# One of the last five output pieces of a hybrid block: scaled by ScalarE and added in DRAM onto an early written residual

## The chip, the cores and the metric

The kernel runs on one core of one Trainium2 chip. The metric is the time of one execution on the device in microseconds (us), the median of several runs. A profile of one execution goes with it; all times within the execution are counted from the start of its span.

## What is computed

One layer (DEPTH = 1) of an encoder block on 256 tokens of width 2048, in float32. What matters here is its frame and its last lines:

```python
mix = hybrid_mixer(u, ...)                       # three branches, then m @ w_out
x = x + _rms_norm(mix, norm_mix_post[l])         # the residual x1
hdn = jnp.square(jax.nn.relu(_rms_norm(x, norm_mlp_pre[l]) @ w_mlp_up[l]))
x = x + _rms_norm(hdn @ w_mlp_down[l], norm_mlp_post[l])
```

The output is therefore x1 + y * g4 * r4, where y is the product of the second half of the MLP, g4 the gain of the last norm (one number per column) and r4 the reciprocal root of y's mean square (one number per token).

## The kernel before, in words

Two token tiles (tt = 0 and 1) of 128 tokens each lie on the 128 partitions. All weights come from one DRAM array, wst, in pieces of 128x1024 (512 KB) loaded by SyncE's queue (L162) into three buffers, `raw`; ScalarE makes a rounded copy `whi` (L173), VectorE the rest `wlo` (L175), and TensorE multiplies with both.

The residual x1 (two tiles of 128x2048) is finished in the middle of the program, when the output projection of the mixer is done: `add_mixed` (L1115, VectorE) adds the normed mix to x in pieces of 512 columns. Right behind, `turn` (L1140, TensorE) transposes each piece, `cut` (L1156 on ScalarE, L1154 on VectorE) scales it by the next norm's gain and splits it, and `part` and `rest` (L1167, L1173, TensorE) begin the MLP's first product with it. In this stretch the order of each engine's instructions is written out by hand.

After that x1 is read for its squares (L1305) and then again only at the end. During most of the MLP, GpSimd issues 56 adding transfers from one SBUF tile to another (`dma_add`, L1358), which add 512 KB onto a buffer that is already filled.

The end of the kernel is the loop over four groups g of 512 columns (its body is L1520 to L1534). `tok` gives the last product of the group for tile 0 and then for tile 1. VectorE adds it to y (L1522), ScalarE squares and sums (L1523), VectorE multiplies by the gain (L1526). In the last group r4 follows (`rstd_of`): ScalarE scales the sum (L1095) and GpSimd takes the power -0.5 (L1096). With r4 the output is made in five pieces of 512, 512, 512, 256 and 256 columns, each one instruction on VectorE (L1532, y * r4 + x1, written over x1) and one transfer to DRAM (L1533). Pieces 0, 2 and 4 are sent by SyncE's queue, pieces 1 and 3 by ScalarE's:

```python
for c, w in (0, 512), (512, 512), (1024, 512), (1536, 256), (1792, 256):
    cs = slice(c, c + w)
    V.scalar_tensor_tensor(x1[tt][:, cs], ys[tt][:, cs], r4, x1[tt][:, cs], ALU.mult, ALU.add)
    (nc.scalar if c == 512 or w == 256 and c == 1536 else nc.sync).dma_start(
        out=out[tt * 128:tt * 128 + 128, cs], in_=x1[tt][:, cs])
```

Outside the stretches that are written out by hand a scheduler sets each engine's order from the dependencies and the order in which the code was written, and assigns a semaphore to each DMA in turn. `junk()` gives one of two 128x512 scratch tiles. At the end SyncE waits for all DMAs that are still under way, and the engines meet (L1655).

Of the kernel before, what the change touches and what calls it, by code (L numbers as in the profile page):

```python
# [13 lines left out]
AF = mybir.ActivationFunctionType  # L14
ALU = mybir.AluOpType
# [37 lines left out]
def hybrid_block(ctx, tc, xt, x, gains, params, consts, lora, gup, wst, out):  # L53
    nc = tc.nc
    V, A, G, PE = nc.vector, nc.scalar, nc.gpsimd, nc.tensor
# [10 lines left out]
    def nm(s):  # L66
        uid[0] += 1
        return f"{s}_{uid[0]}"
# [139 lines left out]
    def tok(pks, lag=1, mid=()):  # L208


        ps = [gps(), gps()]
        n = len(pks)
        kept = []

        def prod(hl, k0, tt):
            for w, parts in ((hl[0], (0, T)), (hl[1], (0,))):
                for k in (k0, k0 + 1):
                    for part in parts:
                        c = part + tt * 128
                        PE.matmul(ps[tt], pks[k][:, c:c + 128], w[:, (k - k0) * 512:(k - k0) * 512 + 512],  # L220
                                  start=k == 0 and part == 0 and w is hl[0], stop=w is hl[1] and k == n - 1)

        for k0 in range(0, n, 2):
            hl = wnext()
            if k0 >= n - 2 * lag:
                prod(hl, k0, 0)
                kept.append((hl, k0))
                tick()
                continue
            for w, parts in ((hl[0], (0, T)), (hl[1], (0,))):  # L230
                for k in (k0, k0 + 1):
                    for tt in range(2):
                        for part in parts:
                            c = part + tt * 128
                            PE.matmul(ps[tt], pks[k][:, c:c + 128], w[:, (k - k0) * 512:(k - k0) * 512 + 512],  # L235
                                      start=k == 0 and part == 0 and w is hl[0], stop=False)
                    if w is hl[1] or k == k0:
                        tick(0.7 if w is hl[0] else 0.5)
        yield ps[0]
        for i, (hl, k0) in enumerate(kept):  # L240
            prod(hl, k0, 1)
            tick()
            if i < len(mid):
                mid[i]()
        yield ps[1]
# [841 lines left out]
    def rstd_of(ss, eps, sums):  # L1087

        if sums is None:
            sums = cpool.tile([128, 1], F32, name=nm("ssum"))  # L1090
            V.tensor_reduce(sums, ss[:, 0:3], AX.X, ALU.add)
            V.tensor_scalar(sums, sums, 1.0 / D, eps, ALU.mult, ALU.add)
            return sums
        r = cpool.tile([128, 1], F32, name=nm("rs"))
        A.activation(r, ss[:, 3:4], AF.Identity, scale=1.0 / D, bias=sums)  # L1095
        G.tensor_tensor(r, r, cst[:, 2:3], ALU.pow)  # L1096
        return r
# [5 lines left out]
    x1 = [p2.tile([128, D], F32, tag="x1", name=nm("x1"), bufs=2) for _ in range(2)]  # L1103
    for c in range(0, D, 512):
        for tt in range(2):
            loads.append(lambda tt=tt, c=c: nc.sync.dma_start(out=x1[tt][:, c:c + 512],
                                                              in_=x[tt * 128:tt * 128 + 128, c:c + 512]))
# [3 lines left out]
    def junk():  # L1111
        return p2.tile([128, 512], F32, tag="junk", name=nm("junk"), bufs=2)
# [174 lines left out]
    ys = []  # L1287
# [227 lines left out]
        return [p3.tile([128, HALF], F32, tag="raw2", name=nm("kw"), bufs=6).bitcast(F32R) for _ in range(2)]  # L1515

    home[0] = spare
    for g in range(4):
        gs = slice(512 * g, 512 * g + 512)
        for tt, ps in enumerate(tok(hp, 4 if g == 3 else 1)):  # L1520
            yv = ys[tt][:, gs]
            V.tensor_tensor(yv, yv, ps, ALU.add)  # L1522
            A.activation(junk(), yv, AF.Square, accum_out=ss4[:, tt, g:g + 1])  # L1523
            if g == 3:
                r4 = rstd_of(ss4[:, tt, :], None, sum4[tt])
            V.tensor_tensor(yv, yv, g4[g], ALU.mult)  # L1526
            if g == 2:
                sum4.append(rstd_of(ss4[:, tt, :], eps4[tt], None))
            if g == 3:
                for c, w in (0, 512), (512, 512), (1024, 512), (1536, 256), (1792, 256):  # L1530
                    cs = slice(c, c + w)
                    V.scalar_tensor_tensor(x1[tt][:, cs], ys[tt][:, cs], r4, x1[tt][:, cs], ALU.mult, ALU.add)  # L1532
                    (nc.scalar if c == 512 or w == 256 and c == 1536 else nc.sync).dma_start(  # L1533
                        out=out[tt * 128:tt * 128 + 128, cs], in_=x1[tt][:, cs])  # L1534
# [125 lines left out]
```

## Time and profile before

| | us |
|---|---|
| median of 3 runs | 1508.16 (1507.34 to 1508.66) |
| the profiled execution's own time | 1509.36 |
| its span, from the first to the last instruction | 1507.6 |
| TensorE busy (share of the span) | 1492.0 (99%) |
| VectorE, ScalarE, GpSimd busy | 1206.6, 939.8, 94.5 |
| mean granted TensorE clock | 0.998 |

In the views, PE is TensorE's matmul and PEld its weight load, DVE is VectorE, ACT ScalarE, POOL GpSimd and SP SyncE; a q behind the name is the engine's sequencer, which also issues its DMAs. A row of the order of time has the start, the duration, the engine, the line, the operation, the tile written and those read, the shapes, the count, and in brackets how long the engine stood idle before and what ended that. A row of the windows has the stretch, its length, the busy time (and count) of PE, PEld, DVE, ACT and POOL, the granted clock, the busy share of the 16 DMA engines and the GB/s that they moved. A row of DMA issues has the transfer, the queue, the count, the size and the median time from issue to landing. Rows of the DMA queues have packets, MB and the share of 16 engines' time; q1 is SyncE's queue, q10 ScalarE's, q0 GpSimd's.

### The profile page before, as it was taken

What the parts mean: (1) busy time and instruction counts of PE and PEld (TensorE: products, weight loads), DVE (VectorE), ACT (ScalarE), POOL (GpSimd) and SP (SyncE); (2) the same over time, 40 slices, a digit from 0 to 9 for tenths busy, and PEclk for the clock granted to TensorE, in tenths of its full rate; (3) what the DMA queues carried; (4) which work ended last, traced back from release to release, by engine and by line L of the source; (5) the groups of instructions that cost most, each with busy time, mean ns of one, the idle gap of its engine ahead of it and who ended that gap; (6) DMA issues with size and microseconds to landing.
All of it is one profiled execution on the core that took longest, in us unless ns stands there. A gap on an engine that the chain in (4) does not pass through costs nothing.

```text
span 1507.6 us, 22703 instructions
## 1 busy us (share of the span) xinstructions
PE 1492.0 (99%) x8384; PEld 1254.0 (83%) x8384; DVE 1206.6 (80%) x1673; ACT 939.8 (62%) x1433; POOL 94.5 (6%) x151
## 2 busy tenths in 40 slices
PE   9999999999999999999999999999999999999997
PEld 7888888887788887788888988888888888888886
DVE  7875679895678796476557778998899989999996
ACT  7665677545676445564545766776667666767663
POOL 0021003000001000000000000000000000000000
PEclk9999999999999999999999999999999999999999
DMA  7655454454455465456675768888888888989874
GB/s 263 197 168 184 142 182 154 154 182 163 156 165 177 154 192 186 130 169 196 231 238 159 265 177 254 229 242 273 263 259 258 244 254 248 258 254 258 246 224 152
DMA packets 104687, 312.71 MB, mean 207 GB/s; under 512 B 10240, under 2 KB 12288, under 8 KB 104576
## 3 DMA queue, kind: packets, MB, share of 16 engines
q1 hardware_dynamic: 93968, 279.87, 56.2%
q0 software_dynamic: 8064, 29.36, 10.5%
q10 hardware_dynamic: 2544, 2.03, 0.5%
q8 instruction: 66, 1.08, 0.3%
q14 instruction: 45, 0.37, 0.1%
HBM read 279.77 MB, written 2.10 MB: 187 GB/s over the span
## 4 chain that ended last, share of the span: by engine, by line
PE 89%; DMA 4%; DVE 2%; issue 2%; ACT 2%; POOLq 0%; SPq 0%; DVEq 0%; POOL 0%; ACTq 0%
PE gps L235 27%; PE gps L191 21%; PE gps L195 12%; PE gps L220 7%; PE mps L1378 3%; PE mps L1380 3%; PE mps L1379 3%; DMA raw<-in_wst_dram 2%; PE gps L1380 2%; PE gps L1378 2%; PE gps L1379 2%; DMA raw<-raw 2%; PE gps L197 1%; DVE wlo L175 1%; ACT whi L173 1%
## 5 line engine op out<-in xcount | busy, mean ns | idle before, releaser
L175 DVE TENSOR_TENSOR wlo<-raw,whi 128x1024 fp32r<-128x1024 f32 x576 | 699.0, 1224 | 159.2 <-ACT whi L173 147.3
L173 ACT ACTIVATE whi<-raw 128x1024 fp32r<-128x1024 f32 x576 | 604.1, 1057 | 260.4 <-PE gps L235 76.3
L191 PE MATMUL gps<-pk,whi 128*128 128x512 f32 x1479 | 375.6, 392 | 1.8 <-DVE tmp L1296 1.0
L191 PEld LDWEIGHTS gps<-pk,whi 128*128 128x128 f32 x1479 | 274.2, 188 | 57.9 <-ACT whi L173 2.3
L235 PE MATMUL gps<-whi,pk 128*128 128x512 f32 x1004 | 253.6, 393 | 0.0
L195 PEld LDWEIGHTS gps<-pk,wlo 128*128 128x128 f32 x1582 | 215.6, 190 | 15.6 <-DVE wlo L175 0.7
L195 PE MATMUL gps<-pk,wlo 128*128 128x256 f32 x1582 | 221.1, 283 | 0.1
L235 PEld LDWEIGHTS gps<-whi,pk 128*128 128x128 f32 x1004 | 186.6, 188 | 39.8 <-issue 1.0
L235 PE MATMUL gps<-wlo,pk 128*128 128x512 f32 x502 | 138.2, 393 | 0.1
L235 PEld LDWEIGHTS gps<-wlo,pk 128*128 128x128 f32 x502 | 93.2, 188 | 20.0 <-DVE wlo L175 0.5
L1378 PE MATMUL mps<-whi,fm 128*128 128x512 f32 x224 | 88.8, 396 | 0.8 <-ACT whi L173 0.6
L1295 ACT ACTIVATE tmp<-gps 128x256 f32<-128x256 f32 x64 | 24.6, 384 | 101.4 <-PE gps L197 99.5
L1379 PE MATMUL mps<-whi,fm 128*128 128x512 f32 x224 | 87.8, 392 | 0.0
L1380 PE MATMUL mps<-wlo,fm 128*128 128x512 f32 x224 | 87.6, 391 | 0.0
L1358 POOL DMA_DIRECT2D raw<-raw x56 | 48.8, 872 | 573.1 <-DVE raw L1355 279.5
L1355 DVE TENSOR_TENSOR raw<-raw,raw 128x1024 f32<-128x1024 f32 x56 | 68.5, 1222 | 0.8
L1378 PE MATMUL gps<-whi,fm 128*128 128x512 f32 x168 | 65.9, 392 | 0.0
L1380 PE MATMUL gps<-wlo,fm 128*128 128x512 f32 x168 | 65.9, 392 | 0.0
L1379 PE MATMUL gps<-whi,fm 128*128 128x512 f32 x168 | 65.5, 390 | 0.0
L220 PE MATMUL gps<-whi,pk 128*128 128x512 f32 x224 | 60.8, 393 | 0.0
L1380 PEld LDWEIGHTS mps<-wlo,fm 128*128 128x128 f32 x224 | 42.1, 188 | 9.7 <-DVE wlo L175 0.2
L1378 PEld LDWEIGHTS mps<-whi,fm 128*128 128x128 f32 x224 | 42.4, 189 | 8.9 <-ACT whi L173 2.9
(346 smaller groups left out, 1726.6 us busy)
## 6 DMA issues: line engine op xcount, KB each, us to landing
raw<-in_wst_dram SPq DMA_DIRECT2D x516, 512.0 KB, 4.4
raw<-raw POOLq DMA_DIRECT2D x56, 512.0 KB, 6.8
x<-in_xt_dram SPq DMA_DIRECT2D x8, 256.0 KB, 6.7
x<-in_x_dram SPq DMA_DIRECT2D x8, 256.0 KB, 4.7
raw<-in_wst_dram SPq DMA_DIRECT2D x4, 256.0 KB, 4.9
g<-in_gains_dram SPq DMA_DIRECT2D x4, 256.0 KB, 4.8
pk<-in_gains_dram SPq DMA_DIRECT2D x4, 256.0 KB, 6.9
out_dram<-x SPq DMA_DIRECT2D x4, 256.0 KB, 2.8
```

The costliest lines, as they stand in the source:

```text
L173: A.activation(hi, raw, AF.Copy)
L175: low = lambda: V.tensor_tensor(lo, raw, hi.bitcast(F32), ALU.subtract)
L191: PE.matmul(ps, hi[:, i * 128:i * 128 + 128], pks[i], start=first and i == 0, stop=False)
L195: PE.matmul(ps[:, 0:T], lo[:, i * 128:i * 128 + 128], pks[i][:, 0:T], start=False, stop=False)
L220: PE.matmul(ps[tt], pks[k][:, c:c + 128], w[:, (k - k0) * 512:(k - k0) * 512 + 512], start=k == 0 and part == 0 and w is hl[0], stop=w is ...
L235: PE.matmul(ps[tt], pks[k][:, c:c + 128], w[:, (k - k0) * 512:(k - k0) * 512 + 512], start=k == 0 and part == 0 and w is hl[0], stop=False)
L1295: A.activation(b, ps[:, T:2 * T], AF.Copy)
L1355: V.tensor_tensor(R[d, a], R[d, a], R[d, b], ALU.add)
L1358: G.dma_start(out=R[d, a], in_=R[d, b], accum_op=ALU.add)
L1378: PE.matmul(Q[f], a, w, start=d == d0 and i == 0, stop=False)
L1379: PE.matmul(Q[f], b, w, start=False, stop=False)
L1380: PE.matmul(Q[f], a, wl, start=False, stop=d == dn and i == 1)
```

## The change

For token tile 1, the first of the five pieces is no longer made by VectorE. The residual x1 of those 512 columns is written to the output in DRAM as soon as it exists, by a transfer of ScalarE's queue. At the end ScalarE multiplies y by r4 into a scratch tile, and a transfer issued by GpSimd adds that tile onto the output in DRAM. Tile 0 and the other four pieces are as before. In the changed file the early write is L1518, the scaling L1535 and the adding transfer L1536; the lines between move down by one (L1522, L1523 and L1526 are L1523, L1524 and L1527), and L1532 and L1533 are L1538 and L1539.

```diff
     home[0] = spare
+    nc.scalar.dma_start(out=out[128:256, 0:512], in_=x1[1][:, 0:512])
     for g in range(4):
...
             if g == 3:
                 for c, w in (0, 512), (512, 512), (1024, 512), (1536, 256), (1792, 256):
                     cs = slice(c, c + w)
+                    if tt and c == 0:
+                        add = junk()
+                        A.activation(add, ys[1][:, cs], AF.Copy, scale=r4)
+                        G.dma_start(out=out[128:256, cs], in_=add, accum_op=ALU.add)
+                        continue
                     V.scalar_tensor_tensor(x1[tt][:, cs], ys[tt][:, cs], r4, x1[tt][:, cs], ALU.mult, ALU.add)
```

The early write is written in the code just ahead of the last loop, but the scheduler moves it up on ScalarE, to the stretch where x1 of tile 1 is finished. There ScalarE's rows are (mps is the transposed piece, pk the split one; a plus marks what the change adds):

```order
 L1156 ACTIVATE pk_7987<-mps_7976,par 128x128
 L173 ACTIVATE kw_8019<-raw_8017 128x1024
+L1518 DMA out_dram<-x_1392_7412 128x512
 L1156 ACTIVATE pk_7915<-mps_8031,par 128x128
 L1156 ACTIVATE pk_7917<-mps_8031,par 128x128
```

The transfer stands between the last copy for the weights (kw) and the first split of tile 1's first piece. No other row moves there, on any engine.

At the end of the program ScalarE's rows before were (y_8772 and x_1391 belong to tile 0, y_8773 and x_1392 to tile 1):

```order
L1533 DMA out_dram<-x_1391_7411 128x512
L1533 DMA out_dram<-x_1391_7411 128x256
L1523 ACTIVATE junk_14504,ss_8165<-y_8773 128x512
L1095 ACTIVATE rs_14506<-ss_8165,ssum_14415 128x1
L1533 DMA out_dram<-x_1392_7412 128x512
L1533 DMA out_dram<-x_1392_7412 128x256
```

and now are:

```order
L1539 DMA out_dram<-x_1391_7411 128x512
L1539 DMA out_dram<-x_1391_7411 128x256
L1524 ACTIVATE junk_14505,ss_8165<-y_8773 128x512
L1095 ACTIVATE rs_14507<-ss_8165,ssum_14416 128x1
L1535 ACTIVATE junk_14511<-y_8773,rs_14507 128x512
L1539 DMA out_dram<-x_1392_7412 128x512
L1539 DMA out_dram<-x_1392_7412 128x256
```

The scaling L1535 has come between r4's input and ScalarE's own two transfers of tile 1.

GpSimd's last rows are now these; L1536 is new, and behind it stands only the end of the program:

```order
L1358 DMA raw_13940<-raw_14003 128x1024
L1358 DMA raw_13938<-raw_14034 128x1024
L1096 TENSOR_TENSOR rs_14466<-rs_14466,cst 128x1
L1096 TENSOR_TENSOR rs_14507<-rs_14507,cst 128x1
L1536 DMA out_dram<-junk_14511 128x512
L1661 UNCONDITIONAL_BRANCH
```

VectorE has one 128x512 instruction of L1532 less for tile 1 (two instead of three), and SyncE one transfer less; the order of all else is as before.

## The prediction

> **What bounds the kernel now.** I read the page first, then the windows of the last 14 us, then the chain of waits and the order of time at the end, then the DMA landings.
>
> ```profile
> span 1507.6 us, 22703 instructions
> PE 1492.0 (99%) x8384; PEld 1254.0 (83%) x8384; DVE 1206.6 (80%) x1673; ACT 939.8 (62%) x1433; POOL 94.5 (6%) x151
> ```
>
> TensorE is busy for all but 15.6 us of the span, so an edit that shortens VectorE is worth nothing in the body. The windows show where TensorE is not the limit.
>
> ```profile
> 1494.00:1498.00 4.00, 4.00 (x18) 3.01 (x17) 3.35 (x6) 0.46 (x3) 0.74 (x1) 1.00 0.25 95
> 1498.00:1504.00 6.00, 0.06 (x1) 0.00 (x0) 4.37 (x8) 1.02 (x3) 0.73 (x1) 0.74 0.68 210
> 1504.00:1507.60 3.60, 0.00 (x0) 0.00 (x0) 0.00 (x0) 0.00 (x0) 0.00 (x0) 0.50 0.46 127
> ```
>
> From 1498 on TensorE has done its work (0.06 us busy), VectorE fills 4.37 of 6 us, and after 1504 no engine computes: only DMA (share 0.46) is left. That tail is all that the edit at the end can touch. In the order of time it looks so (start, duration, engine, line):
>
> ```profile
> 1499.97 0.73 POOL L1096 TENSOR_TENSOR rs<-rs,cst 128x1 f32<-128x1 f32 x1 [4.66 <-ACT rs L1095]
> 1500.73 1.41 DVE L1532 SCALAR_TENSOR_TENSOR x<-y,rs,x 128x512 f32<-128x512 f32 x2 [0.44 <-POOL rs L1096]
> 1501.40 1.41 DVE L1532 SCALAR_TENSOR_TENSOR x<-y,rs,x 128x512 f32<-128x512 f32 x2
> 1502.06 1.14 DVE L1532 SCALAR_TENSOR_TENSOR x<-y,rs,x 128x512 f32<-128x512 f32 x2
> 1503.12 0.48 DVE L1532 SCALAR_TENSOR_TENSOR x<-y,rs,x 128x256 f32<-128x256 f32 x1
> 1501.51 0.33 SPq L1533 DMA_DIRECT2D out_dram<-x  x1
> 1502.18 0.34 ACTq L1533 DMA_DIRECT2D out_dram<-x  x1
> 1502.84 0.33 SPq L1533 DMA_DIRECT2D out_dram<-x  x1
> 1503.24 0.34 ACTq L1533 DMA_DIRECT2D out_dram<-x  x1
> 1503.63 0.33 SPq L1533 DMA_DIRECT2D out_dram<-x  x1
> ```
>
> The five pieces of token tile 1 start on VectorE 0.66 us apart (1500.73, 1501.40, 1502.06; the 256-wide last one at 1503.12), and each is sent 0.04 us after it ends. The landings:
>
> ```profile
> out_dram<-x ACTq DMA_DIRECT2D x1, 256.0 KB, 2.7
> out_dram<-x SPq DMA_DIRECT2D x1, 256.0 KB, 3.0
> out_dram<-x ACTq DMA_DIRECT2D x1, 128.0 KB, 3.3
> out_dram<-x SPq DMA_DIRECT2D x1, 128.0 KB, 3.1
> ...
> SPq L1655 <- DMA out_dram<-x: 2.1, 3, 0.8
> ```
>
> The last piece lands at 1503.63 + 3.1 = 1506.73, SyncE waits for just that (second row), and 1507.6 - 1506.73 = 0.87 us of closing follows. So the end is: last landing + 0.87.
>
> **The change part by part.** *VectorE loses one 512-wide piece.* The next four move 0.66 us earlier; the last plain transfer goes out at 1502.97 and lands at 1506.07 if it still takes 3.1. This bounds the gain: -0.66 us.
>
> *ScalarE gains one scaling.* There was no 128x512 copy from SBUF with a scale per row; the nearest rows are the squares of the same tile and the scaled copy out of PSUM:
>
> ```profile
> L1523 ACT ACTIVATE junk<-y x8: 614/623/634, 1465.5 to 1498.8; 128x512 f32<-128x512 f32 x8
> L972 ACT ACTIVATE vtok<-gps,rstdt x2: 672/681/690, 76.8 to 78.7; 128x512 f32<-128x512 f32 x2
> ```
>
> Between 0.61 and 0.69; I take 0.62, the same operands. It waits for the same result of GpSimd as VectorE, so it runs from 1500.73 to 1501.35. ScalarE's queue then sends piece 1, which VectorE ends at about 1501.47: it is not held up (0.12 us to spare; if the scaling took longer the loss is the excess).
>
> *GpSimd gains one adding transfer, in place of a plain one of SyncE.* GpSimd is idle after 1500.7. It starts at 1501.35 + 0.08 (the gap between ScalarE and GpSimd as before L1096) = 1501.43. No adding transfer into DRAM is in the trace; the nearest are 56 adding transfers between SBUF tiles, 512 KB each:
>
> ```profile
> L1358 POOL DMA_DIRECT2D raw<-raw x56: 860/869/1021, 890.6 to 1443.7; - x56
> ...
> DMA to landing us min/median/max: 4.6/6.8/11.7
> ```
>
> How much of this scales with size? One of them found the DMA engines nearly idle (its issue; the busy tenths of the engines in 40 bins over 1443.6 to 1445.6; its packets in that stretch):
>
> ```profile
> 1443.65 0.87 POOL L1358 DMA_DIRECT2D raw<-raw  x1 [7.33 <-DVE wlo L175]
> ...
> DMA  1101011011000000000000000000009984009994
> ...
> q0 software_dynamic: 32, 0.13, 33.6%
> ```
>
> Its first bytes move at bin 30 (the 8 packets before are another queue's), 1.45 us after the issue, then in rounds some 0.4 us apart with gaps: the time goes by rounds of rows, not by bytes. Packets of two others: of the fastest, which has the engines almost alone (window 922.9 to 925.9), and of one beside plain loads (1421.7 to 1425.7):
>
> ```profile
> q0 software_dynamic: 139, 0.52, 88.4%
> q1 hardware_dynamic: 18, 0.05, 4.2%
> ...
> q0 software_dynamic: 119, 0.46, 57.8%
> q1 hardware_dynamic: 197, 0.67, 45.4%
> ```
>
> That is 139/3.0 = 46 packets per us alone and 119/4.0 = 30 beside others. The page's 8064 packets of q0 over 56 transfers are 144 each, which a 128-row piece has too, of 2 KB rather than 4 KB. The plain pieces' data of before thin out at bin 37 of 40 between 1502.3 and 1506.2, at 1505.9:
>
> ```profile
> DMA  3999999789997999999979899999997667234100
> ```
>
> so now at about 1505.2. If packets set the pace: first bytes at 1501.43 + 1.45 = 1502.88, then 2.3 us beside the plain pieces (70 packets), then 74 packets alone in 1.6 us: 1506.8, and 0.5 us to be confirmed (the fastest one, issued at 921.79, landed at 926.4 and had its data through at 925.9): 1507.3, or 5.9 us from the issue. If bytes do, twice the pace: 1505.8, 4.4 us. The outer bounds: the 4.6 us transfer with its 3.0 us of data halved, 3.1 us (1504.5), and the longest, 11.7 us (1513.1). I take 5.6 us, nearer to the packets' end because of the gaps, and because the sum's far side is now in DRAM: **1507.03**. That is 0.96 after the last plain landing, and 0.30 later than the last landing before.
>
> A page bears on this number. The Trainium skill, "DMA: Bandwidth & Descriptors", section "Anatomy of one DMA — SWDGE (gpsimd) path", fits a transfer of GpSimd's with 2.0 us plus bytes at 436 GB/s; by that, as an estimate, the piece would take 2.6 us after its issue, land at 1504.9 and leave the whole 0.66 us as gain. The trace speaks against it: the fit gives 3.2 us for 512 KB, the 56 adding ones took 3.7 to 10.8 beyond the 0.87 of issuing.
>
> *The early write* is put by the scheduler on ScalarE's queue just ahead of the scaled copies of x1's second tile:
>
> ```profile
> 824.32 0.74 DVE L1115 SCALAR_TENSOR_TENSOR x<-mg,rs,x 128x512 f32<-128x512 f32 x1
> 826.33 0.62 ACT L1156 ACTIVATE pk<-mps,par 128x128 fp32r<-128x128 f32 x2 [2.35 <-PE mps L1140]
> 829.73 0.52 PE L1167 MATMUL gps<-pk,kw 128*128 128x256 f32 x3
> ...
> DMA packets 1, 0.02 MB, mean 4 GB/s; under 512 B 0, under 2 KB 0, under 8 KB 0
> ...
> 840.26 0.94 SPq L1275 DMA_DIRECT2D raw<-in_wst_dram  x2
> ```
>
> It waits for VectorE's piece that ends at 825.06, is issued in 0.34 us (to 825.4) and ScalarE stands idle until 826.33 anyway: 0.9 us of cover. The DMA engines carried one packet from 825 to 829 (fourth row), so its 256 KB hinder no load. Without that cover, ScalarE's eight copies ahead of L1167 would come 0.34 us late, against 829.73 when TensorE takes them: still nothing. It moves the semaphores of all later DMAs by one; a load on SyncE at 840.26 now waits for the early write too, which has long landed by 828.5. Cost 0.
>
> Sum: -0.66 on the plain path, overtaken by the adding transfer at +0.30. Span 1507.6 + 0.3 = 1507.9. The profiled execution took 1509.36 with 1.76 around its span, 1.2 above the median of the runs, 1508.16; I carry the difference to the median: **1508.5**.
>
> **The rivals.** *Full gain.* The adding transfer lands before 1506.07 (under 4.6 us from its issue), and the plain tail sets the end: 1508.16 - 0.66 = 1507.5. For it: half the bytes of the fastest row. Against it: only the fastest of 56 took 4.6, and four plain pieces are in flight beside this one. The fit of the page named above gives this time.
>
> *Starved.* In the slowest of the 56 the DMA engines carried only loads for almost five microseconds after its issue (window 1416.6 to 1421.3: no packet of q0):
>
> ```profile
> q1 hardware_dynamic: 515, 1.10, 76.2%
> ...
> raw<-raw POOLq DMA_DIRECT2D x1, 512.0 KB, 11.7
> ```
>
> If the four plain pieces, issued from 1501.5 to 1503.0, keep the adding one out in the same way, it begins after their data, at about 1505.2, takes 144/46 = 3.1 us, and lands at 1508.8: +2.1. With all of the 11.7 us it lands at 1513.1: +6.4, 1514.5. It is slower by over 0.2% (3.0 us) from a landing 8.3 us after the issue. Against: only 0.79 MB stand ahead, and the first piece alone at the moment of the issue. The Trainium skill, "DMA: Bandwidth & Descriptors", section "Queues, rings and completion order", says that an engine takes turns between its queues packet by packet; by that the adding piece would have its share at once and this rival would fall. The quoted window, with no packet of the adding queue in 4.7 us, does not agree.
>
> *The early write is felt.* ScalarE late by 0.34 us at 826 and passed on: 1508.8. I found no wait that would pass it on. *The change doesn't do what it says*, because the scaling is queued behind something: the order shows nothing between.
>
> **How the numbers follow.** Forecast, adding transfer last with a landing from 0.2 us earlier to 1.5 later than before (1508.0 to 1509.7 on the clock of the median): 0.55. Full gain, 1507.5: 0.25. Starved, +1.5 and more: 0.16, of which over 3.0 us 0.05. Early write felt, or nothing of all this: 0.04. The range takes in full gain with 0.5 us of scatter (the runs lie 0.5 above to 0.8 below their median) and the +2.1 of a begin after the plain data: 1507.0 to 1510.5. Within 0.2%, 3.0 us, about what a measurement of this kernel can tell from no change, lies nearly all: 0.93; faster by more would need more than the 0.66 there is: 0.01; slower 0.06.
>
> **What would show it.** In the profile of the changed kernel: VectorE's last piece ends at 1502.94 and the last plain landing comes about 0.66 us earlier against the end of GpSimd's power; ScalarE's scaling takes 0.62; the adding transfer lands 5.6 us after its issue and SyncE's last wait is for it; 0.87 us follow. At 825 TensorE's times stay. Wrong would be: SyncE's last wait for a plain piece (full gain), no packet of q0 until the plain ones are through (starved), a wait of TensorE at L1167.

## The result, and the profile after

The changed kernel took 1510.58 us (median of 20 runs, 1509.52 to 1512.15), the kernel before 1508.19 (20 runs beside them, 1506.89 to 1511.04). The ratio is 1.0016, 95% interval 1.0009 to 1.0022: 1.4 to 3.3 us slower. The forecast of +0.3 us lies below that interval, and the range of the prediction, up to 1510.5, ends just under the median.

The two profiled executions hide the loss: 1509.63 us for the changed kernel, 1509.36 for before.

```profile
span 1507.8 us, 22702 instructions
```

The spans differ by 0.2 us because the long body, whose code is the same but for the early write, ran faster in the second one: GpSimd's last power (L1096, which yields r4 of tile 1) ended at 1500.70 before and at 1498.02 after. That is scatter: two experiments below, e4 and e8, have the changed kernel's body, and there the same power ended at 1500.56 and 1501.68. Everything that the change does at the end hangs on that instruction, so I measure from its end. **The tail** below is the time from the end of this power to the end of the span: 6.9 us before (1507.6 - 1500.7), 9.8 after. That is +2.9 us by the profiles, and the runs' medians say +2.4.

In the order of time the changed kernel ends so (start, duration, engine, line, and in brackets the idle time before and what ended it; an x2 puts several together):

```profile
1497.29 0.73 POOL L1096 TENSOR_TENSOR rs<-rs,cst 128x1 f32<-128x1 f32 x1 [4.66 <-ACT rs L1095]
1498.05 0.72 ACT L1535 ACTIVATE junk<-y,rs 128x512 f32<-128x512 f32 x1 [0.84 <-POOL rs L1096]
1498.84 0.34 ACTq L1539 DMA_DIRECT2D out_dram<-x  x1
1499.07 0.90 POOL L1536 DMA_DIRECT2D out_dram<-junk  x1 [1.05 <-ACT junk L1535]
1499.38 0.87 DVE L1538 SCALAR_TENSOR_TENSOR x<-y,rs,x 128x256 f32<-128x256 f32 x2
1499.89 0.34 ACTq L1539 DMA_DIRECT2D out_dram<-x  x1
```

The scaling takes 0.72 us, and GpSimd begins its transfer 1.05 us after the power. VectorE is through 2.24 us after the power instead of 2.90: the promised 0.66 us are there. The landings (size, and median us from issue to landing):

```profile
out_dram<-junk POOLq DMA_DIRECT2D x1, 256.0 KB, 5.6
...
out_dram<-x ACTq DMA_DIRECT2D x1, 128.0 KB, 5.1
out_dram<-x SPq DMA_DIRECT2D x1, 128.0 KB, 4.9
```

The adding transfer lands 5.6 us after its issue, as forecast, at 1504.63. But the two last plain pieces, issued about 1 us behind it, now take 5.1 and 4.9 us where they took 3.3 and 3.1. They land last, at 1505.2 (7.14 us after the power; before it was 5.99). And the span does not end 0.87 us after that, but 2.6. The waits of SyncE at the closing (us in total, times, longest) show what it waits for:

```profile
SPq L1661 <- DMA out_dram<-junk: 3.2, 1, 3.2
SPq L1661 <- PEq L1661: 2.4, 2, 1.9
```

After the wait for the adding transfer (first row; the plain pieces behind it cost another 0.8) comes one of 1.9 us for the other engines (longest of the second row). The view puts it down to PE's sequencer, which had long been done. The instructions of the closing line name another (count: shortest/median/longest in ns, first and last start; the longest DRAIN of GpSimd's sequencer is its first). After:

```profile
L1661 POOLq DRAIN  x3: 40/102/7958, 1499.0 to 1507.5; - x3
L1661 SPq DRAIN  x3: 7/7/7, 1505.2 to 1507.3; - x3
```

and before:

```profile
L1655 POOLq DRAIN  x3: 34/93/5422, 1499.9 to 1507.3; - x3
L1655 SPq DRAIN  x3: 7/7/7, 1506.8 to 1507.1; - x3
```

A DRAIN is an instruction of the sequencer at the closing. GpSimd's first one is issued ahead of the end of its last work and lasts for some us beyond it. It ended at 1499.9 + 5.4 = 1505.3 before, 1.4 us ahead of SyncE, which had seen all DMAs by 1506.8, and so it decided nothing. In the changed kernel it lasts until 1499.0 + 8.0 = 1507.0, and SyncE, through at 1505.2, waits for it. The span ends 0.8 us later.

### The profile page after: what moved, and what is told of

It reads as the page before. It is cut to its first block, busy times and chain, and to the rows that moved or that the text cites. A ratio compares the mean times of both kernels' runs of the same rounds, so it can differ in the third digit from the quotient of the medians.

```text
span 1507.8 us, 22702 instructions
## 1 busy us (share of the span) xinstructions
PE 1490.5 (99%) x8384; PEld 1252.9 (83%) x8384; DVE 1206.4 (80%) x1672; ACT 940.7 (62%) x1434; POOL 95.4 (6%) x152
## 4 chain that ended last, share of the span: by engine, by line
PE 94%; DVE 2%; ACT 1%; DMA 1%; issue 1%; POOL 0%; DVEq 0%; SPq 0%; ACTq 0%
PE gps L235 27%; PE gps L191 23%; PE gps L195 13%; PE gps L220 7%; PE mps L1378 3%; PE mps L1379 3%; PE mps L1380 3%; PE gps L1380 2%; PE gps L1378 2%; PE gps L1379 2%; PE gps L197 2%; DVE wlo L175 1%; PE mps L784 1%; PE gps L1167 1%; ACT whi L173 0%
```

## The experiments

Three theories stood against one another, and with them the size of the expected gain:

- **D, the drain**: GpSimd's closing DRAIN ends a fixed time after its last work, 4.66 us after a compute instruction, 2.37 us after the landing of a transfer. An adding transfer at the end lengthens it past SyncE. The two sizes were found on the way: ahead of e3 and e4, D also stood as 7.0 us after the end of the transfer's issue.
- **C, contention**: the adding transfer slows the plain pieces beside it, and the late landing of these makes the loss.
- **E, the early write** costs time in the body or at the end.

In what follows, times with two decimals are us after the end of the power, from the records behind the rows. A kernel that ran once is judged by its tail and its rows, not by its time, since single runs of one kernel lie 4 us apart.

### e1: the early write alone

From the changed kernel; the first piece goes back to VectorE and is written whole.

```diff
-                    if tt and c == 0:
-                        add = junk()
-                        A.activation(add, ys[1][:, cs], AF.Copy, scale=r4)
-                        G.dma_start(out=out[128:256, cs], in_=add, accum_op=ALU.add)
-                        continue
```

> The changed kernel with the early write alone: piece 0 of tile 1 is again made by VectorE and sent by SyncE, and overwrites what was written early. I call tail the time from the end of GpSimd's last power (L1096) to the end of the span: 6.9 us before, 9.8 us with the change. Theory D (the loss sits in GpSimd's closing drain, which the late transfer of GpSimd draws out until it ends last) and theory C (the adding transfer takes DMA time from the plain pieces): tail 6.9, time as before within 0.6 us. Theory E (the early write disturbs the body): tail 6.9, but the time 1.5 to 2.5 us above before.

Measured: 1509.19 against 1508.73, ratio 1.0002 [0.9993, 1.0011]. The interval alone leaves room for up to 1.7 us, but e2 and e6 below have an early write too and are no slower than before. Theory E falls. In the changed kernel the write went out where the order had it (the write on ScalarE's queue; the next split with its wait):

```profile
824.56 0.35 ACTq L1518 DMA_DIRECT2D out_dram<-x  x1
825.80 4.23 ACT L1156 ACTIVATE pk<-mps,par 128x128 fp32r<-128x128 f32 x16 [2.35 <-PE mps L1140]
```

ScalarE's wait for TensorE is the 2.35 us that it was before. The tail of e1 is 7.3 us rather than 6.9, a miss of its own. Its closing:

```profile
L1656 POOLq DRAIN  x3: 34/93/5422, 1499.8 to 1507.6; - x3
L1656 SPq DRAIN  x3: 7/7/7, 1507.0 to 1507.3; - x3
```

GpSimd's DRAIN ends at 1499.8 + 5.4 = 1505.2, no later than before. SyncE comes to its own DRAIN at 1507.0, 0.5 us after the last landing (1503.47 + 3.0 = 1506.5), where before it took 0.1. SyncE tests the semaphores of the DMAs one after another, some 0.06 us each; in this trace the last transfer's semaphore was tested second of nine, with seven others behind it. The early write had shifted which DMA has which semaphore. That is 0.4 us in one trace, and not told from nothing by the runs.

### e2: all but the adding transfer

From the changed kernel; leaves y's share of the first piece out of the output.

```diff
                         A.activation(add, ys[1][:, cs], AF.Copy, scale=r4)
-                        G.dma_start(out=out[128:256, cs], in_=add, accum_op=ALU.add)
                         continue
```

> The changed kernel without the adding transfer: the early write and ScalarE's scaling stay, the output of the piece stays x1 alone. D and C alike: nothing of GpSimd's is under way at the end, VectorE has one piece less, the tail is 6.9 - 0.66 = 6.2 us and the time 0.4 to 1.2 us below before. D says besides that GpSimd's closing drain ends 4.7 us after the power, as before. E: time above before.

Measured: 1507.71 against 1508.73, ratio 0.9991 [0.9982, 0.9999]; the tail is 6.2 us, 0.7 less than before. So the gain that the change is after exists, with its forecast size. The closing and the last landings:

```profile
L1660 POOLq DRAIN  x3: 34/102/5419, 1499.3 to 1506.0; - x3
L1660 SPq DRAIN  x3: 7/7/7, 1505.4 to 1505.7; - x3
```

```profile
out_dram<-x ACTq DMA_DIRECT2D x1, 128.0 KB, 3.2
out_dram<-x SPq DMA_DIRECT2D x1, 128.0 KB, 3.0
```

The plain pieces take 3.2 and 3.0 us again. GpSimd's DRAIN, which now stands behind the power, ends at 4.66 and SyncE is through at 5.41: even with the gain taken, the DRAIN after a power stays hidden, with 0.75 us to spare.

### e3: a plain transfer of GpSimd's

From before; the first piece of tile 1 is made by VectorE and sent, plain, by GpSimd instead of SyncE.

```diff
-                    (nc.scalar if c == 512 or w == 256 and c == 1536 else nc.sync).dma_start(
+                    (G if tt and c == 0 else nc.scalar if c == 512 or w == 256 and c == 1536 else nc.sync).dma_start(
```

> The kernel before, but piece 0 of tile 1 is sent by GpSimd, as a plain transfer, no adding and no early write. D: the drain is long after any late transfer of GpSimd; it ended 7.0 us after the issue in the changed kernel, so it ends about 8.7 us after the power and the tail is 9.2 to 9.6 us. C: it is the adding that costs, so the tail stays at 6.9 to 7.2 us.

Measured (one run, 1509.95): tail 7.4 us, which fits neither expectation. The power, the transfer and the closing:

```profile
1500.09 0.73 POOL L1096 TENSOR_TENSOR rs<-rs,cst 128x1 f32<-128x1 f32 x1 [4.66 <-ACT rs L1095]
1501.90 0.62 POOL L1533 DMA_DIRECT2D out_dram<-x  x1 [1.09 <-DVE x L1532]
```

```profile
out_dram<-x POOLq DMA_DIRECT2D x1, 256.0 KB, 3.0
```

```profile
L1655 POOLq DRAIN  x3: 40/102/5377, 1501.9 to 1507.9; - x3
```

It lands at 1501.90 + 3.0 = 1504.9, and the DRAIN ends at 1501.9 + 5.4 = 1507.3: 2.37 us after the landing by the records, as in the changed kernel (1504.63 to 1507.00). After the end of the issue it is 4.7 us here, so a fixed 7.0 from there falls. Here it ends at 6.44 and SyncE is through at 6.61, so the two are level. No accumulation is needed for the longer DRAIN; a transfer of GpSimd's that lands late does it.

### e4: an adding transfer of 2 KB

From the changed kernel; adds four columns only, and leaves the other 508 without y's share.

```diff
-                        G.dma_start(out=out[128:256, cs], in_=add, accum_op=ALU.add)
+                        G.dma_start(out=out[128:256, 0:4], in_=add[:, 0:4], accum_op=ALU.add)
```

> The changed kernel with the adding transfer cut to 4 of the 512 columns (2 KB in all; the rest of the piece stays x1). It moves next to nothing. C: the plain pieces are free again, tail 6.2 us. D with a drain that runs a fixed 7.0 us from the end of the issue: tail 9.7 us. D with a drain that ends 2.4 us after the transfer has landed: landing 2 to 3 us after the issue, tail 6.2 to 7.2 us.

This run parts C from D: with 2 KB there is next to nothing to contend with. Measured (one run, 1510.02): tail 7.7 us. Its issue, landing and closing:

```profile
1501.61 0.90 POOL L1536 DMA_DIRECT2D out_dram<-junk  x1 [1.05 <-ACT junk L1535]
```

```profile
out_dram<-junk POOLq DMA_DIRECT2D x1, 2.0 KB, 3.5
```

```profile
L1661 POOLq DRAIN  x3: 40/102/5891, 1501.6 to 1508.0; - x3
L1661 SPq DRAIN  x3: 7/7/7, 1506.0 to 1507.7; - x3
```

The last plain piece lands at 5.33, as good as without a transfer (5.26 in e2), and SyncE is through at 1506.0. Yet the span waits for the DRAIN to 1501.6 + 5.9 = 1507.5, which is 6.92, again 2.38 after the landing at 4.54. The landing came 3.5 us after the issue, not 2 to 3, so the tail lies above the expected range as well. Contention gone, it is still 0.8 us longer than before. So D decides: at this place even an adding transfer of 2 KB ends the kernel later than before.

### e5: a late compute instruction on GpSimd, no transfer

From before; GpSimd gets a one-column multiplication that has to wait for VectorE's last piece.

```diff
                         out=out[tt * 128:tt * 128 + 128, cs], in_=x1[tt][:, cs])
+    G.tensor_tensor(cst[:, 3:4], x1[1][:, 2047:2048], cst[:, 2:3], ALU.mult)
```

> The kernel before with one more instruction of GpSimd at the very end: a 128x1 product of the last column of tile 1's output, written to an unused column, so that it can only start when VectorE's last piece is done, 2.9 us after the power. No DMA of GpSimd. So far GpSimd's closing drain ended 4.66 us after the power where GpSimd sent nothing late, and 2.37 us after the landing where it did. If the 4.66 counts from GpSimd's last compute instruction: that ends at about 3.7, the drain at 8.3 and the tail is 9.1 us. If it counts from something else (the landing of other engines' transfers, a fixed time in the program): tail 6.9 us.

Measured (one run, 1509.09): tail 8.6 us, not the 9.1 that D had forecast: for 9.1 the instruction would have to end 3.7 us after the power, and it took only 0.19 us and ended at 3.17.

```profile
1501.69 0.19 POOL L1535 TENSOR_TENSOR cst<-x,cst 128x1 f32<-128x1 f32 x1 [2.98 <-DVE x L1532]
```

```profile
L1656 POOLq DRAIN  x3: 34/102/4884, 1501.7 to 1507.1; - x3
L1656 SPq DRAIN  x3: 7/7/7, 1504.8 to 1506.8; - x3
```

SyncE is through at 1504.8, as early as before (6.12 after the power). The DRAIN lasts to 1501.7 + 4.9 = 1506.6, 4.66 us after the instruction's end: the same 4.66 as after the power. An instruction of 0.19 us, with no transfer and nothing to contend for, lengthens the tail by 1.7 us. That shows the drain by itself.

### e6: the whole change on token tile 0

From the changed kernel; early write, scaling and adding transfer are those of tile 0, whose power comes 5.4 us ahead.

```diff
-    nc.scalar.dma_start(out=out[128:256, 0:512], in_=x1[1][:, 0:512])
+    nc.scalar.dma_start(out=out[0:128, 0:512], in_=x1[0][:, 0:512])
...
-                    if tt and c == 0:
+                    if not tt and c == 0:
                         add = junk()
-                        A.activation(add, ys[1][:, cs], AF.Copy, scale=r4)
-                        G.dma_start(out=out[128:256, cs], in_=add, accum_op=ALU.add)
+                        A.activation(add, ys[0][:, cs], AF.Copy, scale=r4)
+                        G.dma_start(out=out[0:128, cs], in_=add, accum_op=ALU.add)
```

> The same change made to token tile 0 instead of tile 1: its first piece is written early, scaled by ScalarE and added by GpSimd, some 5.4 us earlier than in the changed kernel; all five pieces of tile 1 are as before. D: the adding transfer lands before or about 1 us after tile 1's power, the drain ends by 4.7 us after it as before and is covered; tail 6.9 to 7.1 us, time within 0.7 us of before, though the kernel has the same instructions as the changed one. A loss that comes from the adding itself, from ScalarE's scaling or from the early write would stay: time 1.5 to 2.5 us above before.

Measured: 1507.83 against 1508.16, ratio 0.9996 [0.9988, 1.0005]; the tail is 6.9 us, that of before.

```profile
1493.85 0.90 POOL L1536 DMA_DIRECT2D out_dram<-junk  x1 [1.05 <-ACT junk L1535]
1497.44 0.73 POOL L1096 TENSOR_TENSOR rs<-rs,cst 128x1 f32<-128x1 f32 x1 [2.69 <-ACT rs L1095]
```

```profile
out_dram<-junk POOLq DMA_DIRECT2D x1, 256.0 KB, 5.2
```

```profile
L1661 POOLq DRAIN  x3: 40/93/5526, 1497.4 to 1504.8; - x3
L1661 SPq DRAIN  x3: 7/7/7, 1504.3 to 1504.6; - x3
```

The same transfer, landing at 1493.85 + 5.2 = 1499.05 or 0.9 after tile 1's power, costs nothing: the DRAIN ends at 1502.9, ahead of SyncE at 1504.3. It gains nothing either, since VectorE has no last piece to be rid of there. What costs in the changed kernel is where the transfer stands, not that it exists.

### e7: the share of GpSimd as a compute instruction

From before; ScalarE scales a 256-wide piece, GpSimd adds it to x1, and SyncE or ScalarE send it plain. The piece goes first, so that GpSimd is through early.

```diff
-                for c, w in (0, 512), (512, 512), (1024, 512), (1536, 256), (1792, 256):
+                for c, w in ((1536, 256), (0, 512), (512, 512), (1024, 512), (1792, 256)) if tt else ((0, 512), (512, 512), (1024, 512), (1536, 256), (1792, 256)):
                     cs = slice(c, c + w)
-                    V.scalar_tensor_tensor(x1[tt][:, cs], ys[tt][:, cs], r4, x1[tt][:, cs], ALU.mult, ALU.add)
+                    if tt and c == 1536:
+                        part = junk()
+                        A.activation(part[:, 0:256], ys[1][:, cs], AF.Copy, scale=r4)
+                        G.tensor_tensor(x1[1][:, cs], part[:, 0:256], x1[1][:, cs], ALU.add)
+                    else:
+                        V.scalar_tensor_tensor(x1[tt][:, cs], ys[tt][:, cs], r4, x1[tt][:, cs], ALU.mult, ALU.add)
```

> The kernel before, with one 256-wide piece of tile 1 taken off VectorE in another way: ScalarE scales it, GpSimd adds x1 in SBUF and ScalarE's queue sends it first; no DMA of GpSimd. VectorE ends 0.4 us earlier. If GpSimd's drain runs 4.66 us from its last compute instruction (ending about 1.4 us after the power), it ends at 6.1 and the tail is 6.8 to 6.9: no gain, the drain has taken the place of the landings. If it does not count from there: last landing 5.6, tail 6.4 to 6.5 us, time 0.4 us below before.

Measured: 1508.0 against 1508.16, ratio 0.9997 [0.9987, 1.0006]; tail 6.8 us. This was the attempt at a version that beats both kernels, and it is only level with the one before.

```profile
1499.83 0.75 POOL L1535 TENSOR_TENSOR x<-junk,x 128x256 f32<-128x256 f32 x1 [0.62 <-ACT junk L1534]
```

```profile
L1660 POOLq DRAIN  x3: 34/102/5442, 1499.8 to 1505.7; - x3
L1660 SPq DRAIN  x3: 7/7/7, 1505.0 to 1505.5; - x3
```

```profile
L1537 DVE SCALAR_TENSOR_TENSOR x<-y,rs,x x9: 472/746/1212, 1493.9 to 1501.7; 128x512 f32<-128x512 f32 x6, 128x256 f32<-128x256 f32 x3
```

GpSimd's addition ends at 1.36, the DRAIN 4.66 later at 6.02, and SyncE is through at 5.82: the drain is the end again, by 0.2 us. And one 128x512 piece of VectorE took 1.21 us instead of 0.75 (last row), the one that ran beside GpSimd's addition. VectorE's last piece ends 2.97 us after the power, no earlier than the 2.90 of before: all that it was spared went back that way.

### e8: the same transfer without adding

From the changed kernel; the transfer overwrites the early write instead of adding to it, so x1's share is missing there.

```diff
-                        G.dma_start(out=out[128:256, cs], in_=add, accum_op=ALU.add)
+                        G.dma_start(out=out[128:256, cs], in_=add)
```

> The changed kernel with GpSimd's last transfer as a plain one (it overwrites the early write with the scaled piece, so x1 is missing there). Same bytes written, no reading of DRAM. It tells how much of the 5.6 us to landing and of the plain pieces' delay (last plain landing 7.14 us after the power in the changed kernel, 5.3 without the transfer) is the adding. D: the drain ends 2.37 us after the landing whatever that is; with a landing 3 us after the issue, at 4.1, the tail is 7.3 us. C: the plain pieces end at 5.9 to 6.4 as without adding.

Measured (one run, 1510.87): tail 7.4 us.

```profile
1502.74 0.62 POOL L1536 DMA_DIRECT2D out_dram<-junk  x1 [1.06 <-ACT junk L1535]
```

```profile
out_dram<-junk POOLq DMA_DIRECT2D x1, 256.0 KB, 3.2
...
out_dram<-x ACTq DMA_DIRECT2D x1, 128.0 KB, 3.9
out_dram<-x SPq DMA_DIRECT2D x1, 128.0 KB, 3.7
```

```profile
L1661 POOLq DRAIN  x3: 40/102/5617, 1502.7 to 1508.8; - x3
```

Same place, same size: 3.2 us to land against 5.6 with the addition, and the DRAIN ends at 1502.7 + 5.6 = 1508.3, 2.38 after the landing. So of the tail's 9.8 us, 2.3 (9.76 - 7.43) are the addition itself, passed on through the DRAIN. The plain pieces take 3.9 and 3.7 us beside it, 5.1 and 4.9 beside the adding one: C is real, but it is not what ends the kernel.

### The ten kernels side by side

All in us after the end of the power, except the tail, which is rounded to tenths:

| kernel | GpSimd's last work ends or lands | its DRAIN ends | SyncE through | tail |
|---|---|---|---|---|
| before | power, 0.00 | 4.66 | 6.13 | 6.9 |
| changed | adding 256 KB, 6.61 | 8.98 | 7.29 | 9.8 |
| e1 | power, 0.00 | 4.66 | 6.55 | 7.3 |
| e2 | power, 0.00 | 4.66 | 5.41 | 6.2 |
| e3 | plain 256 KB, 4.07 | 6.44 | 6.61 | 7.4 |
| e4 | adding 2 KB, 4.54 | 6.92 | 5.48 | 7.7 |
| e5 | 128x1 operation, 3.17 | 7.83 | 6.12 | 8.6 |
| e6 | adding 256 KB, 0.9 | 4.75 | 6.15 | 6.9 |
| e7 | 128x256 addition, 1.36 | 6.02 | 5.82 | 6.8 |
| e8 | plain 256 KB, 4.27 | 6.65 | 6.13 | 7.4 |

In each row the tail is the later of the two columns before it plus 0.8. In each row the DRAIN ends 4.66 after a compute instruction, or 2.37 to 2.38 after the landing of a transfer where that is later. The one exception is small: in e6 it ends 4.75 after the power, 0.09 later than that, and no run shows why.

## Why the prediction was wrong

The change did turn out slower, as forecast, but along another path than the forecast has, and by 2.4 us instead of 0.3. The parts that held, or nearly:

- *VectorE loses one piece.* 0.66 us forecast, 0.66 measured; alone (e2) it shortens the tail by 0.7 us.
- *The early write* cost nothing: ratio 1.0002 [0.9993, 1.0011] in e1.
- *The adding transfer takes 5.6 us.* 5.6 measured, but this is partly luck. By packets the prediction had the first bytes 1.45 us after the issue, 3.9 us of data and 0.5 to be confirmed, 5.9 in all (the rounds of its first row are 0.3 us apart rather than 0.4, which entered no sum). In the changed kernel the first packet came 2.1 us after the issue, and a window of 3.2 us (1501.1 to 1504.3) holds all of them; the two misses nearly cancel. Nor does the number of packets alone set the pace, as the prediction read it: e4's 2 KB went as 144 packets too, and a window of 0.6 us (1503.5 to 1504.1) holds them. The packets of the two transfers, first the changed kernel's:

```profile
q0 software_dynamic: 144, 0.26, 61.3%
...
q0 software_dynamic: 144, 0.00, 38.6%
```

- *The fit behind the rival of full gain.* The fit in the Trainium skill, "DMA: Bandwidth & Descriptors", section "Anatomy of one DMA — SWDGE (gpsimd) path", gives 2.6 us for 256 KB as an estimate. Counted from the end of the issue, as the prediction does, the plain transfer agrees with it (3.2 - 0.62 = 2.6 in e8, 3.0 - 0.62 = 2.4 in e3), and the adding one does not (5.6 - 0.90 = 4.7).
- *Scaling by ScalarE* was off: 0.72 us, where the prediction took 0.62 and had 0.69 as the upper bound. GpSimd's issue began 0.29 us after the scaling instead of 0.08, so the transfer was issued 1.05 us after the power instead of 0.73. Worth 0.3 us, the larger part of it this gap.

**The step that failed** is "So the end is: last landing + 0.87." It was read off the kernel before, where it is true, and applied to a kernel in which GpSimd has work at the end. The 0.87 us (0.90 by the records) cover only what follows SyncE's wait. A second condition stood beside it all along, GpSimd's DRAIN, with a slack of 1.4 us that I did not look up: the row was in the trace, under the closing line, lasting 5.4 us. I counted GpSimd "idle after 1500.7" when its DRAIN still ran to 1505.3. In the changed kernel the DRAIN ended at 8.98 and SyncE was through at 7.29, so the span ended 2.6 us after the last landing instead of 0.87.

A second step failed with no effect on the end: "lands at 1506.07 if it still takes 3.1". The pieces behind the adding transfer took 4.9 and 5.1 us, so the plain pieces landed last, 1.77 us later against the power than that step has them (7.14 against 5.37). The forecast that the adding transfer lands last, and the rival in which it is starved, both had the wrong victim: it was the plain pieces that were held up. The window that the prediction quotes against turns between the queues shows only that no packet of the adding queue moved in it, not that one was ready.

How the forecast tail of 7.2 us (1507.03 - 1500.70 + 0.87) becomes 9.8: +0.3 because the transfer is issued later and so lands at 6.61 instead of 6.33, and +2.3 because 3.15 us follow that landing and not 0.87, 2.37 to the end of the DRAIN and 0.78 of closing. The late plain pieces have no part in this sum, since SyncE was through with them 1.7 us ahead of the DRAIN. Had they alone set the end, the loss would have been 8.0 (7.14 + 0.87) - 6.9 = 1.1 us; the drain makes it 2.9.

What stays open: why the DRAIN takes 2.37 us after a landing and 4.66 after an instruction, what sets the pace of the adding transfer, and why the runs' medians show 2.4 us where the tails of two profiles show 2.9. The interval, 1.4 to 3.3, holds both.

## What to carry to other kernels

At the end of these kernels all engines meet, and each has its own condition: look up when every engine's closing DRAIN ends, and how much slack it has, before giving an engine that was idle the last piece of work. Here GpSimd was the engine that had to end early: a compute instruction of its own 4.7 us, the landing of a transfer of its own 2.4 us, before SyncE had seen all DMAs, and that decided more than how long the work took. Where the same code runs ahead of the change, measure from an instruction that both kernels have near the end; the spans here differ by 0.2 us and the tails by 2.9.

## What the runs showed of the hardware

- GpSimd's closing DRAIN ended 4.66 us after its last compute instruction, whether that was a power of 0.73 us, a 128x1 product of 0.19 or a 128x256 addition of 0.75 (4.75 in e6, where an adding transfer landed 0.9 us after the power), and 2.37 to 2.38 us after the landing of its last transfer, plain or adding, 2 or 256 KB (four kernels). The span ended 0.75 to 0.78 us after the later of this DRAIN and SyncE, in all ten kernels.
- Adding into DRAM made a 256 KB transfer of GpSimd's take 5.6 us instead of 3.2 to land, and its issue 0.90 instead of 0.62. Even 2 KB took 3.5 us. The last piece sent behind it landed in 4.9 us, in 3.7 behind a plain transfer of GpSimd's and in 3.0 without one.
- While GpSimd added two tiles (e7), a VectorE instruction with two inputs in SBUF took 1.21 us instead of 0.75. That agrees with the Trainium skill, "SBUF — State Buffer", section "Who interferes with whom": a VectorE instruction with two inputs in SBUF contends with a GpSimd instruction that reads SBUF.
